# A two-layer decoder trunk in float32: boundaries between sub-layers reordered, matmul operands moved by some bytes, first transfers made smaller

## The chip, the cores and the metric

The kernel runs on one core of one Trainium2 chip. The metric is the device time of one execution in microseconds (us); lower is better.

## The reference

A decoder trunk of two layers over 256 tokens of width 2048, all in float32. Each layer has three sandwich-normalised sub-layers on the residual stream `h`:

```python
for l in range(DEPTH):                                   # DEPTH = 2
    xn = rms_norm(h, mix_pre_g[l])
    proj = jnp.einsum('bsd,dc->bsc', xn, w_in[l])        # 2048 x 4176
    ...                                                  # three groups of heads
    h = h + rms_norm(jnp.einsum('bsc,cd->bsd', mix, w_out[l]), mix_post_g[l])
    xa = memory_attention(rms_norm(h, x_pre_g[l]), rms_norm(mem, mem_g[l]), x_wq[l], x_wkv[l], x_wo[l])
    h = h + rms_norm(xa, x_post_g[l])
    ff = swiglu(rms_norm(h, f_pre_g[l]), f_w_gu[l], f_w_down[l])   # 2048 -> 2 x 5632 -> 2048
    h = h + rms_norm(ff, f_post_g[l])
```

Every weight is used once, so it is read from HBM once (about 445 MB in all).

## The kernel before

**Products.** Each large product is made of three products of float32r operands: an operand is split into `hi` (its rounded copy, ScalarE, L208) and `lo` (the rest, VectorE, L209), and hi*hi, hi*lo and lo*hi are added up in PSUM. There are three forms. `mm_t` (L394) holds 128x128 blocks of weights in TensorE and streams the 256 tokens of the turned activations through them; `mm_w` (L413) does the same for the FFN's hidden layer, with the hi and the lo half of the activations streamed in one instruction of 512 columns for the weights' hi half and 256 columns for their lo half; `mm_n` (L431) holds blocks of activations and streams 256 to 512 columns of weights.

**Weights.** `plan` (L264) lists the weights in the order of use, `loaded` (L320) issues their DMAs on the SP queue into a ring of three raw buffers, `splits` (L337) cuts them into a ring of three hi and three lo tiles, and `prefetch(n)` (L359) issues splits until n of them are ready. `weights` (L372) hands them to the three forms and pumps the side generators after each. With `hold`, in the last block of columns of a closing projection, fewer are issued ahead, so that ScalarE and VectorE come to the closing arithmetic sooner.

**Boundaries.** `project_out` (L653) multiplies into five blocks of output columns (three of 512, two of 256). For each it fetches the gain's slice with a POOL-queue DMA into one of two `gb` buffers; `evac` squares the PSUM tile for the norm's sum and multiplies it by the gain into `og`. The next norm's gain and the turn of the residual stream come in `residual` (L610): `row_rsqrt` (eleven small VectorE instructions), then per pair of 128-column chunks `add` (H += og * r, VectorE), `turn_x` (L587: four TensorE transposes into one PSUM tile `xtp`, and two `split`s with a per-column gain: ScalarE to `xh`, VectorE to `xl`). The next projection starts on the first chunks while the later ones are turned. Three boundaries are *bare*: nothing else is left for TensorE between them (cross-attention to FFN in both layers, FFN to the second layer's mixing). There `warm(n)` (L444) issues n matmuls on constants whose result nobody reads, and `begin` sets a manual schedule (instructions stay in program order on VectorE and ScalarE) until the first block is through.

**Place in memory.** In the built program the turned activations (`x`, `mx`) start at byte 37,248 of each partition, the hi and lo tiles of the weights at 110,976 to 131,456 in steps of 4,096, and the hidden layer `hx` at 153,024. A block of 128 columns is 512 bytes. Below, *distance* means the start of the streamed operand minus the start of the held block that is loaded next, modulo 512 bytes: 0 for `x` and `mx` against weights in either role, and -64 for weights streamed against `hx`.

**Names in the rows.** `raw`, `hi`, `lo`: weights; `acc`: the PSUM tiles of the products; `xtp`: the PSUM tile of a turn; `H`: the residual stream; `og`: the sub-layer's output; `gb`: the slice of gain; `sqj`, `sso`, `ssr`, `rs_r`: squares, their sums and the inverse root; `wz`: constants for `warm`.

Of the kernel before, what the change touches and what calls it, by code (L numbers as in the profile page):

```python
# [58 lines left out]
def trunk(ctx: ExitStack, tc, a, onehot, out):  # L59
# [204 lines left out]
    def plan():  # L264
# [7 lines left out]
        for l in range(L):  # L272
# [8 lines left out]
            yield spec(rows(w_in, C_CU, 512), KD, 512, None if l else [(0, 2), (2, 2), (4, 4), (8, 4), (12, 4)])  # L281
# [305 lines left out]
    def turn_x(src, c, xh, xl, gain):  # L587

        p = ps3.tile([P, 512], F32, tag="tp", name="xtp")
        for j in range(2):  # L590
            for t in range(2):
                nc.tensor.transpose(p[:, j * 256 + t * P:j * 256 + (t + 1) * P],  # L592
                                    src[:, t, (c + j) * P:(c + j + 1) * P], ident)
        for j in range(2):
            split(xh[:, c + j, :], xl[:, c + j, :], p[:, j * 256:(j + 1) * 256], gcol(gain[0], gain[1], c + j, KD))
# [14 lines left out]
    def residual(og, ss, evac, nxt, res, bare):  # L610


        evac()
        r = row_rsqrt(ss)
        if bare:
            warm(24)
        yield
        res["x"] = xh, xl, _ = new_x("x")

        def add(c, n):  # L620
            f = slice(c * P, (c + n) * P)
            for t in range(2):
                nc.vector.scalar_tensor_tensor(H[:, t, f], og[:, t, f], r[:, t:t + 1], H[:, t, f],
                                               op0=ALU.mult, op1=ALU.add)

        add(0, 2)
        turn_x(H, 0, xh, xl, nxt)
        if bare:
            warm(5)
            prefetch(2)  # L630
        yield
        add(2, 2)
# [20 lines left out]
    def project_out(nk, xh, xl, og, gain, add=False, first=None):  # L653


        ss = sm.tile([P, 2, len(TAIL)], F32, tag="sso", name="sso", bufs=2)
        for g, (c0, cols) in enumerate(TAIL):
            last = g == len(TAIL) - 1
            gb = wk.tile([P, 512], F32, tag="gb", name="gb", bufs=2)
            nc.gpsimd.dma_start(gb[:, :cols], gain[c0:c0 + cols].partition_broadcast(P))  # L660
            tiles = mm_n(nk, cols, *(first if first and g == 0 else (xh, xl)), hold=last)

            def evac(tiles=tiles, g=g, c0=c0, cols=cols, gb=gb, last=last):
                for t in range(2):
                    d, p = og[:, t, c0:c0 + cols], tiles[t][:, :cols]
                    if add:
                        nc.vector.tensor_tensor(d, p, d, op=ALU.add)
                        square(d, ss[:, t, g:g + 1])
                        (nc.vector if last else nc.gpsimd).tensor_tensor(d, d, gb[:, :cols], op=ALU.mult)
                    else:  # L670
                        square(p, ss[:, t, g:g + 1])
                        nc.vector.tensor_tensor(d, p, gb[:, :cols], op=ALU.mult)
# [4 lines left out]
    def last_residual(og, ss, evac):  # L677

        evac()
        r = row_rsqrt(ss)  # L680
        for g in range(4):
            for t in range(2):
                f = slice(g * 512, (g + 1) * 512)
                if g == 1:
# [5 lines left out]
                nc.sync.dma_start(out[0, t * P:(t + 1) * P, f], H[:, t, f])  # L690


    def fetch_x(i):
        nc.sync.dma_start(H[:, :, i * 512:(i + 1) * 512],
                          x[0, :, i * 512:(i + 1) * 512].rearrange("(t p) f -> p t f", p=P))

    def initial(res):

        res["x"] = xh, xl, _ = new_x("x")
        for c in range(0, KD, 2):  # L700
            if c % 4 == 0 and 0 < c < 12:
                fetch_x(c // 4 + 1)
# [6 lines left out]
    fetch_x(0)  # L709
    for _ in range(1):  # L710
        in_raw.append(next(loads))
    fetch_x(1)
    for _ in range(2):
        in_raw.append(next(loads))
# [7 lines left out]
    for l in range(L):  # L722
# [352 lines left out]
        mxx = new_x("mx")[2]  # L1075
# [44 lines left out]
        begin(residual(og, oss, evac, ("x_pre_g", l), nx, False), 2, -1)  # L1120
# [37 lines left out]
        def x_turn(s):  # L1158
            t = kp.tile([P, 2, 256], F32, tag="ptX", name="ptX", bufs=4)
# [6 lines left out]
            xt.append(t)  # L1166
# [5 lines left out]
        def x_values(h):  # L1172

            p = ps2.tile([P, 512], F32, tag="lg", name="pvx")
            for j in range(2):
                for k in range(2):
                    mm(p[:, j * 256:(j + 1) * 256], vX[:, k, (h + j) * P:(h + j + 1) * P], xt[h + j][:, k, :],
# [14 lines left out]
        oss, evac = project_out(4, cx[:, 0], cx[:, 1], og, a["x_post_g"][l])  # L1192
        nx = {}
        begin(residual(og, oss, evac, ("f_pre_g", l), nx, True), 3, 0)
# [7 lines left out]
        og = xp.tile([P, 2, D], F32, tag="x", name="og")  # L1202
        nh = FH // P // 2
        for hf in range(2):
# [48 lines left out]
            else:  # L1253
                oss, evac = project_out(nh, hh, hl, og, a["f_post_g"][l], True)
        if l < L - 1:
            cur = {}
            begin(residual(og, oss, evac, ("mix_pre_g", l + 1), cur, True), 3, 0)
# [26 lines left out]
```

## Time and profile before

| | us |
|---|---|
| median of 3 runs | 2496.99 (2495.71 to 2498.8) |
| the profiled execution | 2494.86 |
| its span, first to last instruction | 2493.2 |
| TensorE busy in it | 2435.0 |
| VectorE, ScalarE, POOL busy | 1460.2, 1231.1, 268.8 |
| mean granted TensorE clock | 0.993 |

The profile gives each engine's busy time, its instructions in order of time with the idle time ahead of them and what ended it, and tables of stretches. A matmul's recorded duration runs past the start of the next, since matmuls are pipelined; the pace of a stage is the distance from start to start, which is a stretch divided by the instructions that start in it. A table of stretches also counts the one or two that were begun before the stretch.

### The profile page before, as it was taken

The page shows a single profiled execution, that of the slowest core. Times are in us where ns is not written, and L with a number is a line of the kernel's source. Part 1 is how long each engine was busy: PE and PEld are TensorE (multiplying, and loading weights), DVE is VectorE, ACT ScalarE, POOL GpSimd, SP SyncE. Part 2 cuts the span into 40 slices and gives each one's busy share as a digit, 9 for nine tenths or more (in the row PEclk, how much of TensorE's full clock was granted, in tenths as well). Part 3 has the DMA queues.
Part 4 walks back from the last instruction along what each step waited for, and adds up shares of the span by engine and source line. Part 5 has one row for each costly group of instructions (what it writes and reads, how often), then busy time and mean ns, then how long its engine had stood idle before and what let it go on. Part 6 is the DMA issues. An engine that isn't in the chain of part 4 may idle for free.

```text
span 2493.2 us, 37577 instructions
## 1 busy us (share of the span) xinstructions
PE 2435.0 (98%) x15142; PEld 2170.7 (87%) x15142; DVE 1460.2 (59%) x2272; ACT 1231.1 (49%) x1915; POOL 268.8 (11%) x218
## 2 busy tenths in 40 slices
PE   9999999899999999999989999998999999999997
PEld 8999789888888988888889987998888889888887
DVE  5676767555554455555456767675555544555555
ACT  5655645454444444444355655454544444444443
POOL 0010120001110011111100102200011100111111
PEclk9999999999999999999999999999999999999999
DMA  7654575455555555555644555644555556555564
GB/s 262 216 182 144 188 226 175 132 168 186 186 187 188 189 196 186 186 187 191 206 133 136 183 152 177 217 164 136 169 186 186 187 189 198 187 186 186 186 196 134
DMA packets 362867, 452.95 MB, mean 182 GB/s; under 512 B 8970, under 2 KB 280772, under 8 KB 362692
## 3 DMA queue, kind: packets, MB, share of 16 engines
q1 hardware_dynamic: 360628, 444.23, 54.1%
q0 software_dynamic: 2016, 6.29, 1.3%
q8 instruction: 119, 1.95, 0.3%
q14 instruction: 56, 0.46, 0.1%
q10 hardware_dynamic: 48, 0.02, 0.0%
HBM read 444.72 MB, written 5.79 MB: 181 GB/s over the span
## 4 chain that ended last, share of the span: by engine, by line
PE 79%; issue 11%; DVE 5%; ACT 3%; DMA 1%; POOL 1%; SPq 0%; DVEq 0%; ACTq 0%; POOLq 0%
PE acc L203 75%; DVE lo L209 2%; ACT hi L208 1%; POOL mh L212 1%; DMA gb<-in_x_post_g_dram 1%; ACT sqj L579 1%; PE ixp L203 1%; PE lga L203 0%; ACT x L214 0%; DVE mx L209 0%; PE xtp L592 0%; PE pva L203 0%; DMA H<-in_x_dram 0%; PE pvb L203 0%; DVE x L215 0%
## 5 line engine op out<-in xcount | busy, mean ns | idle before, releaser
L209 DVE TENSOR_TENSOR lo<-raw,hi 128x1024 fp32r<-128x1024 f32 (+2 forms) x838 | 1004.6, 1200 | 808.8 <-ACT hi L208 806.4
L203 PE MATMUL acc<-x,hi 128*128 128x512 f32 (+2 forms) x4800 | 1309.1, 345 | 0.0
L208 ACT ACTIVATE hi<-raw 128x1024 fp32r<-128x1024 f32 (+2 forms) x838 | 858.0, 1026 | 890.2 <-PE acc L203 814.6
L203 PE MATMUL acc<-x,lo 128*128 128x256 f32 x3680 | 995.1, 283 | 21.0 <-DVE lo L209 17.4
L203 PEld LDWEIGHTS acc<-x,hi 128*128 128x128 f32 (+1 forms) x4800 | 828.8, 191 | 109.9 <-issue 2.0
L203 PEld LDWEIGHTS acc<-x,lo 128*128 128x128 f32 x3680 | 699.5, 190 | 38.5 <-DVE lo L209 17.8
L203 PE MATMUL acc<-hi,hx 128*128 128x512 f32 (+1 forms) x1760 | 451.6, 347 | 0.0
L203 PEld LDWEIGHTS acc<-hi,hx 128*128 128x128 f32 x1760 | 304.1, 187 | 49.3
L203 PE MATMUL acc<-lo,hx 128*128 128x512 f32 (+1 forms) x880 | 304.6, 347 | 0.0
L203 PEld LDWEIGHTS acc<-lo,hx 128*128 128x128 f32 x880 | 164.8, 187 | 24.2
L1234 POOL TENSOR_TENSOR u<-u,rbh 128x512 f32<-128x512 f32 x40 | 51.9, 1297 | 1004.3 <-DVE u L429 1004.3
L203 PE MATMUL acc<-hi,mx 128*128 128x512 f32 (+1 forms) x576 | 149.7, 347 | 7.0 <-ACT mx L208 5.2
L203 PEld LDWEIGHTS acc<-hi,mx 128*128 128x128 f32 x576 | 100.4, 191 | 21.0 <-ACT mx L208 6.2
L203 PE MATMUL acc<-hi,x 128*128 128x384 f32 (+1 forms) x384 | 109.0, 359 | 0.0
L1209 POOL TENSOR_TENSOR g<-g,u 128x512 f32<-128x512 f32 x44 | 92.7, 2106 | 135.7 <-ACT g L1219 132.6
L203 PE MATMUL acc<-lo,mx 128*128 128x512 f32 (+1 forms) x288 | 99.1, 344 | 0.0
L214 ACT ACTIVATE x<-xtp,gT 128x256 fp32r<-128x256 f32 x96 | 44.0, 470 | 91.0 <-PE xtp L592 64.0
L203 PEld LDWEIGHTS acc<-hi,x 128*128 128x128 f32 x384 | 70.0, 188 | 6.9 <-issue 2.0
L215 DVE SCALAR_TENSOR_TENSOR x<-xtp,gT,x 128x256 fp32r<-128x256 f32 x96 | 45.1, 481 | 41.4 <-ACT x L214 40.7
L203 PE MATMUL acc<-lo,x 128*128 128x384 f32 (+1 forms) x192 | 68.8, 358 | 0.0
L203 PEld LDWEIGHTS acc<-lo,mx 128*128 128x128 f32 x288 | 54.9, 191 | 6.2
L427 ACT ACTIVATE g<-acc 128x256 f32<-128x256 f32 x80 | 30.4, 380 | 59.4 <-PE acc L203 59.4
(244 smaller groups left out, 2000.2 us busy)
## 6 DMA issues: line engine op xcount, KB each, us to landing
raw<-in_f_w_gu_dram SPq DMA_DIRECT2D x160, 1024.0 KB, 5.0
raw<-in_f_w_down_dram SPq DMA_DIRECT2D x76, 1024.0 KB, 5.0
raw<-in_w_out_dram SPq DMA_DIRECT2D x30, 1024.0 KB, 5.3
raw<-in_w_in_dram SPq DMA_DIRECT2D x50, 512.0 KB, 4.7
raw<-in_w_in_dram SPq DMA_DIRECT2D x23, 1024.0 KB, 5.3
raw<-in_x_wkv_dram SPq DMA_DIRECT2D x16, 1024.0 KB, 4.8
raw<-in_f_w_gu_dram SPq DMA_DIRECT2D x32, 512.0 KB, 4.6
raw<-in_w_in_dram SPq DMA_DIRECT2D x12, 960.0 KB, 5.1
```

Of the source, the lines that this page charges most:

```text
L203: return nc.tensor.matmul(o, lhsT=lhsT, rhs=rhs, start=start, stop=stop, skip_group_check=True)
L208: nc.scalar.activation(hi, src, AF.Copy)
L209: eng.tensor_tensor(lo, src, hi.bitcast(F32), op=ALU.subtract)
L212: nc.gpsimd.tensor_scalar(hi, src, scale, None, op0=ALU.mult)
L214: nc.scalar.activation(hi, src, AF.Copy, scale=scale)
L215: nc.vector.scalar_tensor_tensor(lo, src, scale, hi.bitcast(F32), op0=ALU.mult, op1=ALU.subtract)
L427: nc.scalar.activation(dst[:, b, :], t[:, 256:512], AF.Copy)
L579: nc.scalar.activation(q[:, :src.shape[-1]], src, AF.Square, accum_out=red)
L1209: nc.gpsimd.tensor_tensor(g, g, u, op=ALU.mult)
L1234: nc.gpsimd.tensor_tensor(u, u, two(fnx["rb"]), op=ALU.mult)
```

## The change

1. **Weights ahead.** `hold` leaves two splits ready at the end of a closing projection instead of one; at a bare boundary a third is issued after the adds of chunks 4 to 7.
2. **Closing scales resident.** The gains of the cross-attention's and the FFN's closing norms are fetched whole, into `gX` and `gF`, long ahead. The multiplication of the last block by the gain moves behind the inverse root and the first adds (`rest`); after the FFN it goes to POOL.
3. **A bank per turned chunk.** `turn_x` uses two PSUM tiles of two pools for the two chunks of a pair. The adds of chunks 8 to 15 go to ScalarE (scale) and POOL (add): `add_beside`. The step order changes. `warm(24)` and `warm(5)` become one `warm(38)`.
4. **Operands placed.** `new_x` takes an offset; `x` then starts that many bytes below the distance 0 to the weights: 32 for the mixing and cross-attention inputs, 0 for `mx`, 256 (first layer) and 128 (second layer) for the FFN input. A gap of 448 bytes and `gF` put `hx` at distance 0.
5. **First transfers.** The first fetch of x is 256 columns instead of 512, the first weights one block of rows instead of two (then three).
6. `ptX` tiles share the `mp` buffers; the last residual adds run by token half, and one output DMA is issued from ScalarE.

```diff
-            yield spec(rows(w_in, C_CU, 512), KD, 512, None if l else [(0, 2), (2, 2), (4, 4), (8, 4), (12, 4)])
+            yield spec(rows(w_in, C_CU, 512), KD, 512, None if l else [(0, 1), (1, 3), (4, 4), (8, 4), (12, 4)])
...
-                prefetch(3 if not hold else 1 if n == nk else 2 if n + len(subs) >= nk else 3)
+                prefetch(3 if not hold or n < nk else 2)
...
-    def new_x(nm):
-        x = xp.tile([P, 2, KD, S], F32R, tag="xx", name=nm)
+    def new_x(nm, off):
+        f = 2 * KD * S
+        x = xp.tile([P, f + 72], F32R, tag="xx", name=nm)[:, 72 - off // 4:72 - off // 4 + f]
+        x = x.rearrange("p (a k t) -> p a k t", a=2, k=KD)
...
-        p = ps3.tile([P, 512], F32, tag="tp", name="xtp")
-        for j in range(2):
+        for j, (pool, tag) in enumerate(((ps3, "tp"), (ps2, "lg"))):
+            p = pool.tile([P, 512], F32, tag=tag, name="xtp")
...
     residual:
-        evac()
+        rest = evac()
         r = row_rsqrt(ss)
         if bare:
-            warm(24)
+            warm(38)
...
+        def add_beside(c, n):
+            f = slice(c * P, (c + n) * P)
+            for t in range(2):
+                nc.scalar.activation(og[:, t, f], og[:, t, f], AF.Copy, scale=r[:, t:t + 1])
+                nc.gpsimd.tensor_tensor(H[:, t, f], H[:, t, f], og[:, t, f], op=ALU.add)
         add(0, 2)
         turn_x(H, 0, xh, xl, nxt)
         if bare:
-            warm(5)
             prefetch(2)
-        yield
         add(2, 2)
+        rest()
+        yield
         turn_x(H, 2, xh, xl, nxt)
-        yield
-        for c in range(4, KD, 4):
-            add(c, 4)
+        add(4, 4)
+        if bare:
+            prefetch(3)
+        yield
+        turn_x(H, 4, xh, xl, nxt)
+        add_beside(8, 4)
+        yield
+        turn_x(H, 6, xh, xl, nxt)
+        yield
+        turn_x(H, 8, xh, xl, nxt)
+        add_beside(12, 4)
+        yield
+        for c in range(10, KD, 2):
             turn_x(H, c, xh, xl, nxt)
-            yield
-            turn_x(H, c + 2, xh, xl, nxt)
             yield
...
     project_out, the last block:
-                        (nc.vector if last else nc.gpsimd).tensor_tensor(d, d, gb[:, :cols], op=ALU.mult)
+                        if not last:
+                            nc.gpsimd.tensor_tensor(d, d, gb, op=ALU.mult)
...
-        res["x"] = xh, xl, _ = new_x("x")
+        res["x"] = xh, xl, _ = new_x("x", 32)
...
+        gX = kp.tile([P, D], F32, name="gX")
+        nc.gpsimd.dma_start(gX, a["x_post_g"][l].partition_broadcast(P))
...
-        begin(residual(og, oss, evac, ("f_pre_g", l), nx, True), 3, 0)
+        begin(residual(og, oss, evac, ("f_pre_g", l), nx, True, (256, 128)[l]), 3, 0)
...
+        nc.gpsimd.memset(fp.tile([P, 112], F32, name="gap"), 0.0)
+        gF = fp.tile([P, D], F32, name="gF")
+        nc.gpsimd.dma_start(gF, a["f_post_g"][l].partition_broadcast(P))
```

**Where instructions move.** On VectorE, at the first layer's boundary from cross-attention to FFN (`gb` and `gX`: the gain; `sso`: sums of squares; `lo`: a split of the FFN's weights), before:

```order
L672 TENSOR_TENSOR og<-acc,gb 128x256
L209 TENSOR_TENSOR lo<-raw,hi 128x1024
L672 TENSOR_TENSOR og<-acc,gb 128x256 x3
L584 TENSOR_REDUCE ssr<-sso 128x2
L499 TENSOR_SCALAR rs_v<-ssr 128x2
```

and with the change:

```order
L693 TENSOR_TENSOR og<-acc,gX 128x256
L209 TENSOR_TENSOR lo<-raw,hi 128x1024
L693 TENSOR_TENSOR og<-acc,gX 128x256
L209 TENSOR_TENSOR lo<-raw,hi 128x1024
L587 TENSOR_REDUCE ssr<-sso 128x2
L499 TENSOR_SCALAR rs_v<-ssr 128x2
```

The last block's two multiplications have left the place ahead of the reduction, and a second split of the next weights stands there.

On the same engine behind the inverse root, where the residual stream is added up (`H`) and turned (`x`), before:

```order
L623 SCALAR_TENSOR_TENSOR H<-og,rs_r,H 128x256 x2
L215 SCALAR_TENSOR_TENSOR x<-xtp,gT,x 128x256 x2
L209 TENSOR_TENSOR lo<-raw,hi 128x1024
L623 SCALAR_TENSOR_TENSOR H<-og,rs_r,H 128x256 x2
L215 SCALAR_TENSOR_TENSOR x<-xtp,gT,x 128x256 x2
L623 SCALAR_TENSOR_TENSOR H<-og,rs_r,H 128x512 x2
L215 SCALAR_TENSOR_TENSOR x<-xtp,gT,x 128x256 x2
L209 TENSOR_TENSOR lo<-raw,hi 128x1024 x2
```

and with the change:

```order
L624 SCALAR_TENSOR_TENSOR H<-og,rs_r,H 128x256 x2
L215 SCALAR_TENSOR_TENSOR x<-xtp,gT,x 128x256 x2
L624 SCALAR_TENSOR_TENSOR H<-og,rs_r,H 128x256 x2
L703 TENSOR_TENSOR og<-acc,gX 128x256 x2
L215 SCALAR_TENSOR_TENSOR x<-xtp,gT,x 128x256 x2
L624 SCALAR_TENSOR_TENSOR H<-og,rs_r,H 128x512 x2
L209 TENSOR_TENSOR lo<-raw,hi 128x1024
L215 SCALAR_TENSOR_TENSOR x<-xtp,gT,x 128x256 x2
```

The split between the first two turns is gone (it was made earlier), the two multiplications by the gain come here, and of the two splits in a row ahead of the fourth turn one comes ahead of the third.

On TensorE at the same boundary, before:

```order
L203 MATMUL acc<-hi,cx 128x256
L448 MATMUL warm<-wz 128x256 x24
L592 MATMUL xtp<-ident,H 128x128 x4
L448 MATMUL warm<-wz 128x256 x5
L203 MATMUL acc<-x,lo 128x256
```

and with the change:

```order
L203 MATMUL acc<-hi,cx 128x256
L448 MATMUL warm<-wz 128x256 x38
L595 MATMUL xtp<-ident,H 128x128 x4
L203 MATMUL acc<-x,lo 128x256
```

The constants' matmuls stand in one group ahead of the first turn, and nothing stands between that turn and the first product.

## Rows read from the trace of the kernel before

**Rows 1.** The page's part 1: busy time, share, instructions of each engine.

```profile
PE 2435.0 (98%) x15142; PEld 2170.7 (87%) x15142; DVE 1460.2 (59%) x2272; ACT 1231.1 (49%) x1915; POOL 268.8 (11%) x218
```

**Rows 2.** Timeline, first boundary to the FFN: start, duration, engine, operation [idle <-releaser].

```profile
474.75 3.04 PE L448 MATMUL warm<-wz 128*128 128x256 f32 x24
...
477.91 0.75 DVE L672 TENSOR_TENSOR og<-acc,gb 128x256 f32<-128x256 f32 x2 [2.67 <-DMA gb<-in_x_post_g_dram]
...
480.69 0.88 DVE L623 SCALAR_TENSOR_TENSOR H<-og,rs_r,H 128x256 f32<-128x256 f32 x2
481.32 0.85 PE L592 MATMUL xtp<-ident,H 128*128 128x128 f32 x4 [3.53 <-DVE H L623]
...
482.73 0.47 PE L203 MATMUL acc<-x,lo 128*128 128x256 f32 x1
```

**Rows 3.** Timelines of PE, ACT and DVE further on at that boundary.

```profile
491.33 1.04 PE L592 MATMUL xtp<-ident,H 128*128 128x128 f32 x8
495.83 0.39 PE L203 MATMUL acc<-x,lo 128*128 128x256 f32 x1 [3.46 <-DVE lo L209]
...
519.56 0.39 PE L203 MATMUL acc<-x,lo 128*128 128x256 f32 x1
519.78 0.28 PE L203 MATMUL acc<-x,hi 128*128 128x256 f32 x1
...
520.50 0.28 PE L203 MATMUL acc<-x,hi 128*128 128x256 f32 x1
...
493.10 0.47 ACT L214 ACTIVATE x<-xtp,gT 128x256 fp32r<-128x256 f32 x1 [0.55 <-DVE x L215]
493.47 1.99 ACT L208 ACTIVATE hi<-raw 128x1024 fp32r<-128x1024 f32 x2
...
494.55 2.36 DVE L209 TENSOR_TENSOR lo<-raw,hi 128x1024 fp32r<-128x1024 f32 x2 [0.46 <-ACT hi L208]
```

**Rows 4.** Table of stretches: from:to, us, PE busy (instructions), granted clock, DMA share, GB/s.

```profile
482.90:486.20 3.30, 3.30 (x16) 0.50 0.00 0
```

**Rows 5.** PE's timeline at the other two bare boundaries: `warm`, and the second block's start.

```profile
1237.51 3.04 PE L448 MATMUL warm<-wz 128*128 128x256 f32 x24
...
1281.07 0.39 PE L203 MATMUL acc<-x,lo 128*128 128x256 f32 x1
...
1715.51 1.72 PE L448 MATMUL warm<-wz 128*128 128x256 f32 x13
...
1760.61 0.38 PE L203 MATMUL acc<-x,lo 128*128 128x256 f32 x1
```

**Rows 6.** Table of stretches: five stages at a steady pace.

```profile
1575.10:1589.30 14.20, 14.20 (x64) 1.00 0.76 232
842.00:867.00 25.00, 25.00 (x223) 1.00 0.65 206
350.00:370.00 20.00, 20.00 (x169) 1.00 0.72 225
760.00:830.00 70.00, 70.00 (x302) 1.00 0.53 182
550.00:700.00 150.00, 150.00 (x860) 1.00 0.57 189
```

**Rows 7.** PE's groups by line and form: count, busy us, mean ns.

```profile
L203 PE MATMUL acc<-x,hi 128*128 128x512 f32 x2560 | 889.9, 396 | 0.0
L203 PE MATMUL acc<-x,hi 128*128 128x256 f32 x2176 | 414.6, 288 | 0.0
L203 PE MATMUL acc<-hi,hx 128*128 128x512 f32 x1056 | 331.8, 394 | 0.0
```

**Rows 8.** Timelines of the first product and of the end, by engine.

```profile
9.51 0.35 PE L203 MATMUL acc<-x,lo 128*128 128x256 f32 x1 [1.30 <-DVE lo L209]
...
2479.48 0.97 DVE L669 TENSOR_TENSOR og<-og,gb 128x256 f32<-128x256 f32 x2 [0.29 <-ACT sqj L579]
...
2483.33 3.42 POOL L686 TENSOR_TENSOR H<-H,og 128x512 f32<-128x512 f32 x2 [15.55 <-ACT og L685]
```

More of the change, by code (lines that the diff above doesn't have):

```diff
@@ L587, in turn_x @@
     def turn_x(src, c, xh, xl, gain):
-        p = ps3.tile([P, 512], F32, tag="tp", name="xtp")
-        for j in range(2):
+        for j, (pool, tag) in enumerate(((ps3, "tp"), (ps2, "lg"))):
+            p = pool.tile([P, 512], F32, tag=tag, name="xtp")
             for t in range(2):
[L592 to L595, printed above, removed]
+                nc.tensor.transpose(p[:, t * P:(t + 1) * P], src[:, t, (c + j) * P:(c + j + 1) * P], ident)
+            split(xh[:, c + j, :], xl[:, c + j, :], p[:, 0:256], gcol(gain[0], gain[1], c + j, KD))
     def pre_norm(res):
@@ L658, in project_out @@
             last = g == len(TAIL) - 1
-            gb = wk.tile([P, 512], F32, tag="gb", name="gb", bufs=2)
-            nc.gpsimd.dma_start(gb[:, :cols], gain[c0:c0 + cols].partition_broadcast(P))
+            if gain.shape[0] == P:
+                gb = gain[:, c0:c0 + cols]
+            else:
+                gb = wk.tile([P, 512], F32, tag="gb", name="gb", bufs=2)[:, :cols]
+                nc.gpsimd.dma_start(gb, gain[c0:c0 + cols].partition_broadcast(P))
             tiles = mm_n(nk, cols, *(first if first and g == 0 else (xh, xl)), hold=last)
@@ L668, in evac, with rest @@
                         square(d, ss[:, t, g:g + 1])
-                        (nc.vector if last else nc.gpsimd).tensor_tensor(d, d, gb[:, :cols], op=ALU.mult)
+                        if not last:
+                            nc.gpsimd.tensor_tensor(d, d, gb, op=ALU.mult)
                     else:
                         square(p, ss[:, t, g:g + 1])
-                        nc.vector.tensor_tensor(d, p, gb[:, :cols], op=ALU.mult)
+                        if not last:
+                            nc.vector.tensor_tensor(d, p, gb, op=ALU.mult)
+                if not last:
+                    return
+                def rest():
+                    for t in range(2):
+                        d, p = og[:, t, c0:c0 + cols], tiles[t][:, :cols]
+                        if add:
+                            nc.gpsimd.tensor_tensor(d, d, gb, op=ALU.mult)
+                        else:
+                            nc.vector.tensor_tensor(d, p, gb, op=ALU.mult)
+                return rest
             if last:
@@ L677, in last_residual @@
     def last_residual(og, ss, evac):
-        evac()
+        rest = evac()
         r = row_rsqrt(ss)
[L681 to L684, printed above, removed]
+        rest()
+        for t in range(2):
+            for c0, n, beside in ((512, 512, True), (0, 512, False), (1024, 512, False), (1536, 512, False)):
+                f = slice(c0, c0 + n)
+                if beside:
                     nc.scalar.activation(og[:, t, f], og[:, t, f], AF.Copy, scale=r[:, t:t + 1])
@@ L689, in last_residual, with fetch_x @@
                                                    op0=ALU.mult, op1=ALU.add)
[L690 to L695, printed above, removed]
+                (nc.scalar if t and beside else nc.sync).dma_start(out[0, t * P:(t + 1) * P, f], H[:, t, f])
+    def fetch_x(c0, n):
+        nc.sync.dma_start(H[:, :, c0:c0 + n], x[0, :, c0:c0 + n].rearrange("(t p) f -> p t f", p=P))
     def initial(res):
-        res["x"] = xh, xl, _ = new_x("x")
+        res["x"] = xh, xl, _ = new_x("x", 32)
         for c in range(0, KD, 2):
             if c % 4 == 0 and 0 < c < 12:
-                fetch_x(c // 4 + 1)
+                fetch_x((c // 4 + 1) * 512, 512)
             turn_x(H, c, xh, xl, ("mix_pre_g", 0))
@@ L708, in trunk @@
     next(g0)
[L709 to L714, printed above, removed]
+    fetch_x(0, 256)
+    in_raw.append(next(loads))
+    fetch_x(256, 256)
+    in_raw.append(next(loads))
+    fetch_x(512, 512)
+    in_raw.append(next(loads))
     warm(12)
```

22 lines of the change are left out of this document (12 added, 10 removed).

## The prediction

> **What bounds the kernel now.** The page's part 1 comes first: TensorE is busy for 2435.0 of 2493.2 us [rows 1], and no other engine for 60% of the span. So time can come from two places only: the stretches in which TensorE stands still or runs at half clock, and the pace of its matmuls where it runs without a gap.
>
> The standing time is found in the timeline of a bare boundary [rows 2]. At the first one, real work ends at 474.75, where the 24 warm matmuls begin. VectorE then waits 2.67 us for the gain's slice, still on its way by DMA, multiplies for 0.75, and the eleven small instructions of the inverse root and the first adds follow. TensorE waits 3.53 us for H, turns, runs five more warm matmuls, and the first product starts at 482.73: 7.98 us after the warm start. Further on it waits again, 3.46 us from the second pair of turns to 495.83, for a `lo` that is split only then [rows 3]: ScalarE and VectorE had the turned chunks first, and there each copy of a second chunk waits for VectorE on the first (0.55 us), because both lie in one PSUM tile. The table of stretches shows the clock at 0.50, the 1.2 of the two levels 1.2 and 2.4 GHz, right behind the idle time [rows 4]. From the warm start to the second block's first product, 519.56, 44.8 us pass for 192 matmuls [rows 2, 3]. These run at 0.12 us each, six starts from 519.78 to 520.50 [rows 3], so they need 23.0 us. The other two boundaries take 43.6 and 45.1 us [rows 5].
>
> The pace is read from stretches without idle time, less the two instructions begun before each [rows 6]. Hidden layer by down weights, 512 columns (distance -64): 70 us by 300, 233 ns. The same with 256 columns: 25 us by 221, 113 ns. Output projection, distance 0: 512 columns 14.2 us by 62 or 63, about 227 ns; 256 columns 20 us by 167, 120 ns. The FFN's pair of 512 and 256 columns, distance 0: 150 us by 429 pairs, 350 ns. The same instruction differs by up to 7 ns from place to place at full clock, and in opposite senses for 512 and 256 columns.
>
> **The change part by part.**
>
> *Start of a bare boundary (parts 1 to 3).* With the gain resident the wait of 2.67 us goes, and with the multiplications moved 0.75 us more. What is late next: a second split, 1.2 us of VectorE (half of the 2.36 of two [rows 3]), now stands ahead of the reduction, and the squares must be done. I let the reduction start at 476.5, two microseconds earlier than now (477.91 + 0.75 = 478.66). The inverse root takes 2.1 us (478.6 to 480.69 [rows 2]) and the way from there to the first turn 0.63, so H is ready for it at 479.2. The 38 warm matmuls take 38 by 0.12 = 4.6 us and end at 479.4, which is level with it. From the turn's start to the first product it is now 1.41 us with five warm matmuls between [rows 2]; without them and with a copy that starts after two transposes, 1.0. First product: 480.4 instead of 482.73.
>
> *The rest of the first block.* Two splits are ready and the third is issued before it is needed, so the wait of 3.46 us goes, and with both waits the half clock behind them: two such stretches at this boundary, each worth half its 3.4 us. What is left is 23.0 us of products, seven more turns of four transposes at 0.5 (eight in 1.04 [rows 3]), 3.5, and some 0.7 us for each of the first two turns, whose chunks are still being added up: 27.9 us, so 508.3 against 519.56, a gain of 11.2. By the same steps the second boundary, which waits for no DMA and gains only 0.9 at its start, ends 9.7 earlier, and the third 11.5 [rows 5]. The sum is 32.4; I take off 0.1 us for each of the 24 handovers: **-30**. Ends: half of it, -15, if the split's turn on ScalarE and VectorE stays what products wait for, and -36 with no wait left at the early turns.
>
> *POOL's adds.* Four adds of 512 columns at each boundary at 1.71 us [rows 8] are 6.8 us on POOL, wanted some 10 us after their inputs are there: nothing. If they slow VectorE beside them, 2 us at each of three boundaries: ends 0 and +6. The fetches of gX and gF stand ahead of them on POOL's queue, but in memory that is long free.
>
> *First transfers (part 5).* The first product waits for `lo`, at 9.51 [rows 8]. Half the bytes come first and the split is half as wide: about 0.6 us each on ScalarE and VectorE for 1.1 to 1.2. The following blocks come no sooner. **-1.5**, ends -2.5 and +0.5. *End (part 6).* The inverse root need not wait for two multiplications (from 2479.48, 0.97 us [rows 8]); the squares end about 0.4 before them: **-0.4**, ends -1 and +1, since POOL takes their place.
>
> *hx at distance 0 (part 4).* 1056 hi and half as many lo products of 512 columns [rows 7], 1584 by (227 - 233) ns, are -9.5 us. The tail's two blocks of 256 against three of 512 make 1056 of those, by (120 - 113), +7.4. **-2**, ends 0 and -9.5.
>
> *x off distance 0 (part 4).* The trace has no row of -32, 128 or 256. `mm_t`: 2176 hi products and half as many lo, 3264 of 256 columns [rows 7], of which about 3000 leave distance 0. Nearest rows: 120 ns at 0, 113 at -64 (with the roles exchanged); I take the middle, -3.5 ns: **-10**, ends 0 and -21. `mm_w`: 2560 pairs [rows 7]. At best 227 + 113 = 340 ns, at worst 233 + 120 = 353, now 350. I take 347, a little over the middle: **-7**, ends -25 and +8. `mm_n` on x (some 550 instructions of 384 and 512 columns): nothing, ends -4 and +4.
>
> Here a rule speaks against the change. The rows say that the same streamed block takes 113 or 120 ns by where it lies [rows 6]. The Trainium skill, "TensorE: Matmul & The Clock Gate", section "Step-by-step: what each phase is for", gives TensorE two independent SBUF read ports and says that loading the next tile's weights "doesn't steal SBUF read bandwidth from the running matmul". By that rule the place of an operand is worth nothing and the sum lacks the last three terms; the rows disagree with it, unless the difference comes from something else in those stages, and that is the first rival.
>
> The sum: -30 - 1.5 - 0.4 - 2 - 10 - 7 = -50.9 from the profiled execution's 2494.86, which is 2.1 under the median shown: **2444 us**.
>
> **The rivals.** *Placement does nothing.* The 7 ns between stages would come from what else runs there, not from the distance. For: stages also differ in DMA load, 0.53 to 0.76 [rows 6], and in which operand is held. Against: 512 columns go the other way than 256 within the same stages. Only the boundaries, the start and the end remain, -31.9: 2463.
>
> *The boundaries give half.* The third split needs a buffer of the ring of three, which is free only when the first split's products are through; the wait for `lo` comes back, shorter, at the next pair. For: ScalarE and VectorE each work 2.3 to 2.4 us for two chunks (a split, two copies), near TensorE's 3.4. Against: that is still less. -15 - 1.9 - 19 = -35.9: 2459.
>
> *Slower: the FFN's pair loses.* The hidden layer streams two runs of 256 columns, 16 KB apart, and the offsets 256 and 128 were tried in no row. Each ns on the pair costs 2.56 us. With -44 from the rest the pair must rise by 17 ns, to 367, for no change; at 372 (every matmul of it as much above the slowest rows as those are above the fastest) it is 2494.9 - 44 + 56 = 2507. For: the two lengths go in opposite senses. Against: no row is that slow.
>
> *Placement does more.* Both forms go to their best rows, 113 ns and 340: 2494.9 - 33.9 - 21 - 25 = 2415.
>
> That the change does not do what it says is excluded by the order of its instructions.
>
> **How the numbers follow.** Forecast 0.48, placement nothing 0.22, half the boundaries 0.13, more 0.11, the FFN's pair loses 0.06. A measurement of this kernel tells 0.2%, 5 us, from no change. All but the last lie clearly below; of the mixed ends (half the boundaries and a small loss of pace) I put 0.03 within 5 us. Faster 0.92, same 0.03, slower 0.05. The range reaches from the best case, 2414, past "placement nothing" and some loss of pace with it, 2475: what lies outside is the last rival, half the boundaries without any gain of pace, and both placements at their best with a boundary better than I have it.
>
> **What would show it.** Right: some 5.7 us from a bare boundary's warm start to its first product and 33 to 34 to the second block's first; no wait for `lo` of 3 us; no or little half clock there. 227 and 120 ns in the hx products; less than 120 in `mm_t`, less than 350 in the FFN's pair. Wrong: if the hx products stay at 233 and 113, distance is not the cause; if the first block still takes 40 us, the weights are not ahead; if the pair is over 353, the offsets are badly put.

## Result and the profile after the change

| | before | after |
|---|---|---|
| median, us | 2497.26 (2495.71 to 2498.8, 4 runs) | 2463.19 (2460.3 to 2463.72, 4 runs) |
| profiled execution, us | 2494.86 | 2460.3 |
| its span, us | 2493.2 | 2458.6 |

The ratio is 0.9861, 95% interval 0.9844 to 0.9878: 34 us faster. The forecast said 2444 with a range of 2414 to 2475; the time lies in the range, 19 us above the forecast, and within 1 us of the first rival, "placement does nothing". One execution of a kernel below (*Weights not ahead*) had a mean granted clock of 0.555 and took 4006.84 us; that kernel's times are given without it.

Part 1 of the page after, to be held against [rows 1]:

```profile
PE 2419.2 (98%) x15169; PEld 2170.7 (88%) x15169; DVE 1456.6 (59%) x2249; ACT 1240.9 (50%) x1936; POOL 296.8 (12%) x228
```

TensorE lost 15.8 us of busy time. POOL gained 28.0: the adds of chunks 8 to 15 take 34.6, and it fetches fewer slices of gains. ScalarE gained 9.8, VectorE lost 3.6. The rest of the 34.6 us by which the span is shorter, 18.8, is idle time of TensorE that is gone.

**The first boundary.** Timelines of the changed kernel by engine (start, duration, engine, operation, [idle before <-releaser]), against [rows 2, 3]:

```profile
477.71 4.72 PE L448 MATMUL warm<-wz 128*128 128x256 f32 x38
482.27 0.60 PE L595 MATMUL xtp<-ident,H 128*128 128x128 f32 x4
...
483.33 0.39 PE L203 MATMUL acc<-x,lo 128*128 128x256 f32 x1 [0.46 <-ACT x L214]
...
495.25 0.44 PE L595 MATMUL xtp<-ident,H 128*128 128x128 f32 x2 [0.30 <-POOL H L631]
...
512.16 0.28 PE L203 MATMUL acc<-x,lo 128*128 128x256 f32 x1
...
478.97 0.16 DVE L587 TENSOR_REDUCE ssr<-sso 128x2 f32<-128x10 f32 x1
...
484.89 0.75 DVE L703 TENSOR_TENSOR og<-acc,gX 128x256 f32<-128x256 f32 x2
```

The squares' sum (L587) no longer waits for the gain: the multiplication (L703) comes six microseconds behind it. The first product starts 5.62 us after the warm start (7.98 before), the second block 34.45 (44.8 before). No wait of 3.46 us for `lo` is left; the longest is 0.74, at 496.43. The half clock of [rows 4] is gone with the idle time, as the first row of the second table below shows.

**Stretches.** A table of stretches gives for TensorE: from:to, us, busy (instructions), granted clock, DMA share, GB/s. First the kernel before (cross-attention from its first memory product to the warm start; then the three bare boundaries, each from the warm start to the first product of the next kind, with FFN, mixing and FFN behind it; the second half of the FFN's hidden layer, second layer; 480 `mm_t` products of the mixing, with 101 smaller instructions between them that are the same in every kernel):

```profile
371.87:474.75 102.88, 102.88 (x782) 1.00 0.48 161
474.75:746.58 271.83, 261.17 (x1603) 0.99 0.54 177
1237.51:1324.90 87.39, 77.94 (x607) 0.96 0.49 153
1715.51:1987.63 272.12, 261.80 (x1603) 0.98 0.54 176
2109.96:2356.23 246.27, 246.27 (x1410) 1.00 0.57 188
158.92:232.03 73.11, 73.11 (x582) 1.00 0.53 161
```

Then the same places after, with the stretch behind the first product ahead of them and the two kinds of `hx` products behind:

```profile
483.30:486.20 2.90, 2.87 (x24) 1.00 0.04 13
374.02:477.71 103.69, 102.48 (x782) 1.00 0.46 159
477.71:737.16 259.45, 257.27 (x1613) 1.00 0.56 186
1226.31:1303.46 77.15, 73.87 (x616) 1.00 0.53 169
1694.84:1954.56 259.72, 257.51 (x1612) 1.00 0.56 185
2076.00:2323.04 247.04, 247.04 (x1411) 1.00 0.57 188
161.10:233.57 72.47, 72.47 (x582) 1.00 0.53 163
737.16:826.92 89.76, 89.76 (x398) 1.00 0.56 191
826.92:858.60 31.68, 31.68 (x266) 1.00 0.60 192
```

The ledger, after minus before: the three boundaries -12.4, -10.2 and -12.4, so -35.0. Cross-attention +0.8 in each layer (the second layer's stretch is 102.88 and 103.69 too). The `hx` products of a half take 89.8 + 31.7 = 121.4 us instead of 92.4 + 29.9 = 122.3 (396 and 264 at the paces of [rows 6]): -3.6 over four halves. The hidden layer's second half 0.0 and +0.8. All up to the first memory product +2.15 (its starts are 371.87 and 374.02 in the second rows). These make -34.0; the rest, to -34.6, is nearly all the end.

**Two places that got worse.** In the cross-attention, the changed kernel's timelines of PE, DVE and POOL at 382 to 388 us:

```profile
381.63 6.96 POOL L631 TENSOR_TENSOR H<-H,og 128x512 f32<-128x512 f32 x4 [3.80 <-ACT og L630]
...
383.44 1.77 DVE L624 SCALAR_TENSOR_TENSOR H<-og,rs_r,H 128x512 f32<-128x512 f32 x1
385.13 2.31 DVE L209 TENSOR_TENSOR lo<-raw,hi 128x1024 fp32r<-128x1024 f32 x1
...
387.59 0.36 PE L203 MATMUL acc<-mh,lo 128*128 128x256 f32 x1 [1.21 <-DVE lo L209]
```

An add of VectorE and a split take 1.77 and 2.31 us while POOL adds, and TensorE waits for the `lo` tile behind them. And at the start, TensorE's waits in the changed kernel:

```profile
9.10 0.39 PE L203 MATMUL acc<-x,lo 128*128 128x256 f32 x1 [1.05 <-ACT x L214]
...
12.27 0.96 PE L595 MATMUL xtp<-ident,H 128*128 128x128 f32 x7 [1.50 <-DMA H<-in_x_dram]
...
69.45 0.39 PE L203 MATMUL acc<-x,lo 128*128 128x256 f32 x1 [0.70 <-DVE lo L209]
...
106.84 0.39 PE L203 MATMUL acc<-kvn,lo 128*128 128x256 f32 x1
```

The first product comes 0.41 us earlier than [rows 8] have it. The second fetch of x is then waited for, and at 69 us a split stands behind VectorE's work on the lambda constants (small products of the input `a_lambda`). TensorE's waits before 107 us add up to 7.3 us, where they were 5.3, and the first `kvn` product starts 2.2 us later than in the kernel before (104.63).

### The profile page after: what moved, and what is told of

It is laid out like the page before. It is cut to its first block, busy times and chain, and to the rows that moved or that the text cites. A ratio compares the mean times of both kernels' runs of the same rounds, so it can differ in the third digit from the quotient of the medians.

```text
span 2458.6 us, 37634 instructions
## 1 busy us (share of the span) xinstructions
PE 2419.2 (98%) x15169; PEld 2170.7 (88%) x15169; DVE 1456.6 (59%) x2249; ACT 1240.9 (50%) x1936; POOL 296.8 (12%) x228
## 4 chain that ended last, share of the span: by engine, by line
PE 93%; DVE 3%; DMA 1%; ACT 1%; issue 0%; SPq 0%; DVEq 0%; ACTq 0%
PE acc L203 89%; DVE lo L209 1%; PE ixp L203 1%; PE xtp L595 1%; PE lga L203 0%; DVE mx L209 0%; ACT hi L208 0%; DVE H L624 0%; DMA H<-in_x_dram 0%; PE warm L448 0%; PE pva L203 0%; DMA m<-in_mem_dram 0%; PE pvb L203 0%; PE lgx L203 0%; PE pvx L203 0%
## 5 line engine op out<-in xcount | busy, mean ns | idle before, releaser
L203 PEld LDWEIGHTS acc<-x,hi 128*128 128x128 f32 (+1 forms) x4800 | 818.6, 188 | 107.7 <-issue 2.0
L203 PEld LDWEIGHTS acc<-x,lo 128*128 128x128 f32 x3680 | 691.6, 188 | 23.0 <-ACT x L214 9.7
L427 ACT ACTIVATE u<-acc 128x256 f32<-128x256 f32 x80 | 30.4, 379 | 58.5 <-PE acc L203 58.5
```

The source lines that it names most:

```text
L203: return nc.tensor.matmul(o, lhsT=lhsT, rhs=rhs, start=start, stop=stop, skip_group_check=True)
L427: nc.scalar.activation(dst[:, b, :], t[:, 256:512], AF.Copy)
```

## Experiments

The theory after the result: the boundaries brought all of the gain, placement nothing but the `hx` products, and POOL's adds took something back. The rival: placement brings what the forecast gave it, and the boundaries brought half. Times below are medians with the kernel before beside them (2496.8 to 2497.5), and stretches as above. The profiled execution was the fastest of its runs for the changed kernel and three of the variants, and the slowest for two, so stretches are compared with stretches and medians with medians.

### Placement undone

```diff
-begin(residual(og, oss, evac, ("f_pre_g", l), nx, True, (256, 128)[l]), 3, 0)
+begin(residual(og, oss, evac, ("f_pre_g", l), nx, True, 0), 3, 0)
...
-nc.gpsimd.memset(fp.tile([P, 112], F32, name="gap"), 0.0)
+nc.gpsimd.memset(fp.tile([P, 96], F32, name="gap"), 0.0)
```

The three offsets of 32 become 0 likewise.

> Only the placement is undone: x, mx and the FFN input at distance 0, hx at -64 again; boundaries, start and end as changed. Theory 1, the gain is that of the boundaries and the placement is worth the 3.6 us of the hx products alone: 2463 + 3 = about 2466 us, hx at 233 and 113 ns, second half of the FFN's mm_w products 246.3 us in both layers as in both kernels. Theory 2, placement gives the 10 to 19 us of the forecast and the boundaries only some 18: 2473 to 2482 us.

2457.92 us (2457.54 to 2459.52), ratio 0.9843 (0.9828 to 0.9858): no slower without the placement. Its interval overlaps that of the changed kernel, so the 5 us between the medians don't show it to be faster. One thing in the expectation is wrong: the shorter gap does not put `hx` back to -64 but on the other side, to +64. There its products ran as at no place before (512 columns, then 256):

```profile
739.47:830.12 90.65, 90.65 (x398) 1.00 0.55 189
830.12:860.04 29.92, 29.92 (x265) 1.00 0.64 203
```

That is 120.6 us in a half, where distance 0 gave 121.4 and -64 122.3. The second layer's hidden half went back from 247.04 to 246.27. With `hx` at -64 the four halves would take 7 us more, by an estimate from these stretches (122.3 - 120.6 each), which makes some 2465 us, where theory 1 has 2466. Theory 2 falls: 10 to 19 us of placement are not there.

### The adds of chunks 8 to 15 back on VectorE

```diff
 def add_beside(c, n):
-    for t in range(2):
-        nc.scalar.activation(og[:, t, f], og[:, t, f], AF.Copy, scale=r[:, t:t + 1])
-        nc.gpsimd.tensor_tensor(H[:, t, f], H[:, t, f], og[:, t, f], op=ALU.add)
+    add(c, n)
```

> The residual adds of chunks 8 to 15 go back to VectorE everywhere (no ScalarE scale, no POOL add). Theory 1, POOL's adds slow VectorE beside them, and that is what the cross-attention lost: from the last mx product to the first warm matmul 102.9 us as before the change, not 103.7, in both layers, and the lo splits beside the boundary at 1.2 us where one took 2.2; the bare boundaries then either gain the 1.5 us waited at chunks 8 and 9 or lose up to 3 us each for VectorE's four extra adds of 0.74 us. In all 2459 to 2470 us. Theory 2, the cross-attention's loss has another cause (the gain's fetch, another order): it stays at 103.7 us.

2456.55 us (2453.9 to 2458.39), ratio 0.9835 (0.9821 to 0.985). Cross-attention and first boundary, in the table of stretches:

```profile
375.16:477.40 102.24, 102.24 (x782) 1.00 0.49 161
477.40:735.49 258.09, 256.94 (x1613) 1.00 0.57 187
```

VectorE's timeline at that boundary, then POOL's and VectorE's of the changed kernel at the same place:

```profile
492.06 1.40 DVE L624 SCALAR_TENSOR_TENSOR H<-og,rs_r,H 128x512 f32<-128x512 f32 x2
493.38 1.22 DVE L209 TENSOR_TENSOR lo<-raw,hi 128x1024 fp32r<-128x1024 f32 x1
```

```profile
492.67 2.52 POOL L631 TENSOR_TENSOR H<-H,og 128x512 f32<-128x512 f32 x2 [5.74 <-ACT og L630]
497.24 2.12 POOL L631 TENSOR_TENSOR H<-H,og 128x512 f32<-128x512 f32 x1 [2.04 <-ACT og L630]
...
494.11 2.17 DVE L209 TENSOR_TENSOR lo<-raw,hi 128x1024 fp32r<-128x1024 f32 x1 [1.65 <-ACT hi L208]
...
496.99 1.21 DVE L209 TENSOR_TENSOR lo<-raw,hi 128x1024 fp32r<-128x1024 f32 x1
498.12 0.86 DVE L215 SCALAR_TENSOR_TENSOR x<-xtp,gT,x 128x256 fp32r<-128x256 f32 x2
```

With four more adds of its own at each boundary VectorE is through sooner: its last `xl` split ends 28.7 us after the warm start at the first boundary, 30.1 in the changed kernel. The gain is 1.45 us in each cross-attention and 1.3 to 1.4 at each of the three boundaries, 6.9 in all: that is what POOL's help cost. The run takes out ScalarE's scaling together with POOL's adds, and at the bare boundaries the two are not told apart; in the cross-attention TensorE's wait of 1.21 us stands behind the slowed rows of VectorE and is gone here. Instructions whose two tensor inputs both lie in SBUF slow down beside POOL: an add of 128x512 takes 0.70 us here and took 1.77 in the cross-attention above, a split of weights 1.22 here and 2.17 and 2.31 there. The two `xl` splits at 498.12, with one input in PSUM, took 0.86 for both in the middle of POOL's work, no more than the 0.88 they take elsewhere. Which of the two began first decides who is slowed. Of the sixteen splits of weights that ran beside these adds, the three begun ahead of the add kept 1.21 us, as at 496.99, and there the add took 2.12, where those that meet no split take 1.3; the thirteen begun behind it took 1.23 to 2.31. The Trainium skill, "SBUF — State Buffer", section "Who interferes with whom", says so: a VectorE instruction with two SBUF inputs contends with a GpSimd instruction that reads SBUF, and the second one waits. By that rule the adds were not free, and the trace agrees.

### Weights not ahead

```diff
-prefetch(3 if not hold or n < nk else 2)
+prefetch(3 if not hold else 1 if n == nk else 2 if n + len(subs) >= nk else 3)
...
 add(4, 4)
-if bare:
-    prefetch(3)
```

> Splits ahead undone: one split ready at the end of the closing projection and no third split after the adds of chunks 4 to 7; all else as changed. Theory 1, the wait for lo at the second pair of turns is what the first block lost: each bare boundary is longer by 5 to 9 us, with a wait for lo of 2 to 3.5 us at the second pair, 2478 to 2490 us. Theory 2, the separate banks and the moved multiplications carry the gain: 0 to 3 us a boundary, below 2472 us.

2473.69, 2474.79 and 2478.14 us, ratio 0.9916 (0.9896 to 0.9936). The first boundary's stretch:

```profile
478.31:742.28 263.97, 259.00 (x1612) 0.99 0.56 182
```

TensorE's longest wait in it, from its timeline, with the row ahead of it:

```profile
491.17 1.03 PE L595 MATMUL xtp<-ident,H 128*128 128x128 f32 x8
494.83 0.44 PE L595 MATMUL xtp<-ident,H 128*128 128x128 f32 x2 [2.63 <-POOL H L631]
```

4.5, 4.0 and 4.5 us are lost (81.19 and 264.18 at the others), 13.0 in all: below theory 1 and above theory 2. The wait does not come back at `lo`, either. POOL's adds of chunks 8 and on begin 15.2 us after the warm start, 15.0 in the changed kernel, so they are hardly late. But the third split comes at 494.94 (489.45 in the changed kernel), and until then TensorE has no products to run between the turns of chunks 4 to 7 and that of chunk 8 (the changed kernel runs 24 there, from 491.60 to 494.57): it comes to the turn at once and stands there for H. The products behind the waits then run at a granted clock of 0.50, the 1.2 GHz level, 0.21 us from start to start where 0.12 is usual.

### One bank for a pair

```diff
-for j, (pool, tag) in enumerate(((ps3, "tp"), (ps2, "lg"))):
-    p = pool.tile([P, 512], F32, tag=tag, name="xtp")
+p = ps3.tile([P, 512], F32, tag="tp", name="xtp")
...
```

> turn_x puts both chunks of a pair into one PSUM tile again; all else as changed. Theory 1, the copy of a second chunk that waits 0.5 us for VectorE lies on TensorE's path at each of the eight pairs: 3 to 4 us more at each bare boundary (warm start to the first hx product 262 to 263 us where the changed kernel has 259.5), some 2474 us in all. Theory 2, VectorE's own load sets the pace of a boundary and a ScalarE wait costs nothing: under 1 us each, 2463 to 2466 us.

2479.98 us, ratio 0.9931 (0.9917 to 0.9944). The first boundary's stretch:

```profile
479.82:744.18 264.36, 258.61 (x1612) 1.00 0.56 182
```

ScalarE's timeline in it:

```profile
499.69 0.47 ACT L214 ACTIVATE x<-xtp,gT 128x256 fp32r<-128x256 f32 x1 [2.26 <-DVE x L215]
```

4.9, 5.2 (82.37) and 5.0 us (264.71), more than theory 1 had it. The copy of a second chunk waits for VectorE not only 0.55 us as in [rows 3] but up to 2.26, because VectorE may have a split of weights ahead of the first chunk's `lo`; ScalarE's own splits queue behind that copy. The split in question (497.11) took 2.16 us beside POOL's adds; behind one that took 1.23 (501.14) the wait is 1.32. So a part of this price is POOL's.

### Gains fetched late

```diff
-oss, evac = project_out(4, cx[:, 0], cx[:, 1], og, gX)
+oss, evac = project_out(4, cx[:, 0], cx[:, 1], og, a["x_post_g"][l])
...
-rest = evac()
+evac()
 r = row_rsqrt(ss)
```

> Closing gains fetched slice by slice again, and the last block multiplied by the gain ahead of the inverse root, as in the kernel before (after the FFN on POOL, where that kernel used VectorE); all else as changed. Theory 1, the forecast's: the wait of 2.67 us for the slice and 0.75 us of multiplications come back ahead of the first turn at both cross-attention boundaries and 0.9 at the other: 3.4 + 3.4 + 0.9 = some 8 us, 2471 us. Theory 2, a part of it is covered, since the splits issued ahead now stand before the reduction: 3 to 5 us in all, 2466 to 2468 us.

2470.06 us, ratio 0.9894 (0.988 to 0.9907). Stretches of the first and third boundary:

```profile
480.35:743.78 263.43, 259.07 (x1612) 0.99 0.56 182
1700.34:1966.10 265.76, 260.36 (x1612) 0.99 0.56 181
```

The third's waits, from the timelines of VectorE and TensorE:

```profile
1704.96 0.76 DVE L699 TENSOR_TENSOR og<-acc,gb 128x256 f32<-128x256 f32 x2 [3.28 <-DMA gb<-in_x_post_g_dram]
...
1708.37 1.09 PE L595 MATMUL xtp<-ident,H 128*128 128x128 f32 x4 [3.31 <-DVE H L624]
```

4.0 and 6.0 us at the boundaries behind the cross-attention, -0.3 at the other (76.88), which never waited for a slice: 9.8, at two of the three places that theory 1 named and a little above its 8. The profiled execution was the slowest of four; the medians lie 6.9 us apart. At the third boundary the first products behind the wait run at a granted clock of 0.50, which is a part of its 6.0.

### First transfers wide again

```diff
-[(0, 1), (1, 3), (4, 4), (8, 4), (12, 4)]
+[(0, 2), (2, 2), (4, 4), (8, 4), (12, 4)]
...
-fetch_x(0, 256)
+fetch_x(0, 512)
...
```

> The first transfers as in the kernel before: 512 columns of x and two blocks of rows of weights. Theory 1, the narrow ones bring the first product 0.4 us forward and pay for it with a wait of 1.8 us behind the first block; the start of the mixing's mm_n products (118.8 us in the changed kernel, 116.6 before) comes 0 to 1.5 us earlier with the wide ones, and the rest of the 2.2 us is the lambda constants' work, which the new order of instructions puts between two splits. Theory 2, the narrow transfers gain the 1.5 us of the forecast and other things lose 3.7: then the wide ones bring it to 120 us.

2462.59 us (2462.1 to 2462.96). TensorE's first product and first `kvn` product:

```profile
9.52 0.55 PE L203 MATMUL acc<-x,lo 128*128 128x256 f32 x1 [1.30 <-DVE lo L209]
...
106.61 0.39 PE L203 MATMUL acc<-kvn,lo 128*128 128x256 f32 x1
```

Between these two executions the narrow transfers bring 0.42 us at the first product and nothing by 106 us (106.84 with them). Neither is shown to be theirs: in the other kernels with narrow transfers the first product starts anywhere from 8.76 to 10.38, and the `kvn` product from 106.95 to 108.98. The 2 us behind the kernel before (104.63) are there in both, so the transfers alone don't cause them. Waits at the lambda work are a part of them; what moved that work was not tried.

### Other places

```diff
-begin(residual(og, oss, evac, ("f_pre_g", l), nx, True, (256, 128)[l]), 3, 0)
+begin(residual(og, oss, evac, ("f_pre_g", l), nx, True, (64, 32)[l]), 3, 0)
...
-hx = fp.tile([P, 2, nh, S], F32R, tag="hx", name="hx")
+ho = ((416, 320), (192, 0))[l][hf] // 4
+hx = fp.tile([P, 2 * nh * S + 128], F32R, tag="hx", name="hx")[:, ho:ho + 2 * nh * S]
```

The other inputs' offsets change in the same way, and the gap goes. In the first expectation the sign of the places of `hx` and `mx` is again the opposite of what was run: weights minus `hx` was 32, 128, 256 and -64, weights minus `mx` 64 and 32.

> Other places in memory only. hx at distance -32 and -128 (first layer, first and second half) and 256 and 64 (second layer); x at -64 and -48 (mixing, first and second layer), -16 and -96 (cross-attention), -64 and -32 (FFN); mx at -64 and -32. Theory 1, the pace follows the distance whichever operand is held: mx at -64 like hx was, 233 and 113 ns; mm_t at -64 at 113 ns, some 3 us less in 480 products; -32 between the two at 230 and 117; FFN pair at -64 113 + 233 = 346 ns or less, 6 us less over a half. Theory 2, only held activations follow it: mx at -64 at 233 and 113, but mm_t stays at 117 to 120 ns and the FFN's pair at 350 to 352 ns wherever x lies.

> Other places only. Weights minus hx 48 and 80 (first layer), 96 and -192 (second); mx 48 and 96; mixing input -80 and -96, cross-attention -64 and -80, FFN -192 and -16. If only multiples of 64 give full steps, hx at 48, 80 and 96 lies between the values at 32, 64 and 128 (512 columns 229 to 233 ns, 256 columns 113 to 119), -192 reads like 64 and not like 256; mm_t at -80 and -96 is slower than at -64 (over 71.3 us for 480 products); the FFN's pair at -192 and -16 is 350 ns or more, since no place tried so far beat 350.

2469.35 and 2466.6 us, one run each. Two stretches of the first (480 `mm_t` products at -64; the first layer's hidden half with x at -64), and the first of these at -80 in the second:

```profile
161.78:233.06 71.28, 71.28 (x581) 1.00 0.54 166
858.87:1107.30 248.43, 248.43 (x1411) 1.00 0.57 187
```

```profile
161.12:234.03 72.91, 72.91 (x582) 1.00 0.54 163
```

`hx` products, ns each (a stretch divided by its 396 or 264 products):

| weights minus `hx` | -64 | 0 | 32 | 48 | 64 | 80 | 96 | 128 | 256 | -192 |
|---|---|---|---|---|---|---|---|---|---|---|
| 512 columns | 233.3 | 226.7 | 233.3 | 231.8 | 228.9 | 230.0 | 233.3 | 232.4 | 226.8 | 228.9 |
| 256 columns | 113.4 | 120.0 | 116.7 | 116.7 | 113.3 | 118.1 | 120.0 | 118.6 | 120.0 | 117.8 |

Stretches with x streamed, us (the first has 101 other instructions in it):

| x minus weights | 0 | -16 | -32 | -48 | -64 | -80 | -96 | -128 | -192 | -256 |
|---|---|---|---|---|---|---|---|---|---|---|
| 480 `mm_t` | 73.11 | | 72.47 | 72.82 | 71.28 | 72.91 | 72.26 | | | |
| hidden half (704 pairs) | 246.27 | 248.26 | 248.43 | | 248.43 | | | 247.04 | 246.91 | 246.27 |

The held `mx` follows the table at 32 (22.40 us for 192 products of 256 columns, 116.7 ns) but not at 64 (22.62 us, 117.8 ns, where `hx` has 113.3). The place counts for streamed x too, against theory 2 of the first sweep: `mm_t` is best at -64, 1.8 us for 480 products. But the pair is best at 0 and at -256, and theory 1's gain of 6 us at -64 is a loss of 2.2.

### Two versions that put this together

`best1` has VectorE's adds, x at -64 (mixing, cross-attention) and 0 (FFN), `mx` at 32 and `hx` at 64. `best2` has `hx` at 0 again and the narrow blocks' own place. The diffs to the changed kernel, of `best1` and then of what `best2` has besides:

```diff
-begin(residual(og, oss, evac, ("x_pre_g", l), nx, False, 32), 2, -1)
+begin(residual(og, oss, evac, ("x_pre_g", l), nx, False, 64), 2, -1)
...
-nc.gpsimd.memset(fp.tile([P, 112], F32, name="gap"), 0.0)
+nc.gpsimd.memset(fp.tile([P, 96], F32, name="gap"), 0.0)
```

```diff
-hi = ws.tile([P, 1024], F32R, tag="hi", name="hi")
+hi = ws.tile([P, 1024], F32R, tag="hi", name="hi")[:, place:]
...
-yield spec(rows(wd, c0, n), nh, n)
+yield spec(rows(wd, c0, n), nh, n, None, 3 if n == 256 else None, 16 if n == 256 else 0)
```

> The changed kernel with the adds of chunks 8 to 15 on VectorE, the FFN input at distance 0, the mixing and cross-attention inputs at -64, mx at 32 and hx at 64 (weights minus hx). By the stretches measured so far: 6.9 us from the adds, 3.5 from hx, 0.8 from the second layer's FFN, 1.2 us for 480 mm_t products at -64 instead of -32 in each layer, 0.6 for mx in each: 2463 - 15 = about 2448 us. If the parts overlap or the total follows the order of instructions instead, 2453 to 2458 us.

> As the version before (best1), but hx at distance 0, where its 512-column products took 226.7 ns, and the weights of the down projection's two narrow blocks 64 bytes further in their tiles, so that those 256-column products see 64 (113.3 ns). To make room they are split three blocks of rows at a time instead of four. If the pace follows the distance of the very instruction: 89.8 and 29.9 us in each half instead of 90.7 and 29.9, 3.5 us less in all, 2444 us. If the smaller splits (a fourth of the products per handover less) become the wait, or the narrow products follow something else than this distance: 31.7 us or more, 2448 to 2452 us.

`best1`: 2447.54 us (2446.35 to 2447.95), ratio 0.9801 (0.9788 to 0.9815), 15.6 us under the changed kernel, and within 1 us of the 2448 that the stretches of the runs above add up to. The stretch of its first boundary (the one with 480 `mm_t` products took 71.28 us):

```profile
477.98:736.08 258.10, 256.96 (x1613) 1.00 0.57 187
```

`best2`: 2446.95 us (2445.53 to 2447.34), the same. Its two kinds of `hx` products:

```profile
734.78:824.54 89.76, 89.76 (x398) 1.00 0.57 191
824.54:855.64 31.10, 31.10 (x265) 1.00 0.59 186
```

The wide blocks have their 226.7 ns; the narrow ones take 117.8 at the same 64 bytes at which they took 113.3 when `hx` had been moved instead of the weights. It is not a wait where one split hands over to the next: 252 of the 263 steps from start to start are 117 to 119 ns. `mx` at 64 had 117.8 as well, and there nothing was split smaller. The distance modulo 512 bytes is therefore not all that counts; what else does was not found.

## Why the prediction came out as it did

- **Start of a bare boundary and its first block (-30): right.** First product 5.62 us after the warm start at the first and third (5.7 forecast), second block after 34.3 to 35.7 (33 to 34). At the middle one the start brought nothing: 7.11 where 6.84 had been, since TensorE waits 1.12 us for H behind the warm matmuls. To the second block the three gain 10.4, 7.9 and 10.8 us, 29.0. Behind it they gain 1.6 to 2.4 us more, which the forecast left out: at the first boundary 1.4 of it are two waits of 0.7 us for `lo` (at 523.40 and 527.22 in the kernel before). Taken away alone, weights ahead cost 13.0, a bank per chunk 15.1 and resident gains 9.8 us. That is 37.9, more than the 35.0 of all together, so the parts overlap. What the longer `warm(38)` does by itself was not tried.
- **POOL's adds (0, ends 0 and +6): wrong, they cost 6.9.** Two mistakes. The step priced them only at the bare boundaries, though the mixing's `residual` runs them too (2.9 of the 6.9); and it took the lower end. The trace before had a row against it, in the view of the tile `H` (least, median and longest ns), for the six adds of VectorE at the kernel's end, where POOL adds beside them:

```profile
L688 DVE SCALAR_TENSOR_TENSOR H<-og,rs_r,H x6: 739/747/1748, 2482.6 to 2487.9; 128x512 f32<-128x512 f32 x6
```

- **`hx` at distance 0 (-2): right, -3.6.** 226.7 and 120.0 ns, where the forecast had 227 and 120; with the unrounded 6.6 ns both ways, 1584 products gain 10.5 and 1056 lose 7.0.
- **`mm_t` off distance 0 (-10): mis-sized.** The middle between two rows was taken for a place that neither of them showed. At -32 480 products gain 0.64 us, 1.3 ns each, where 3.5 were taken. At -64 the same products gain 1.83, 3.8 ns each: the nearest row's place would have brought the term, the place chosen did not. In the totals even the 0.64 us is lost among waits: the second layer's mixing, from its first `cqh` product (1303.46) to the first memory product (1591.15), took 287.69 us, and 287.73 in the kernel before (1324.90 to 1612.63).
- **The pair (-7): wrong, 0 and +0.8.** At -256 nothing changes, at -128 it is 1 ns slower; none of the six places tried beat 0.
- **First transfers (-1.5): wrong, nothing.** The step priced the wait for `lo` alone. With `lo` early the first product waits for ScalarE's copy of the turned chunk instead (9.10, `ACT x`) and comes only 0.41 us sooner (in the other kernels with narrow transfers between 0.75 sooner and 0.87 later), and then TensorE waits 1.50 for the second fetch of x.
- **End (-0.4): right**, some 0.5 by the ledger. What no step had: the 2 us of new waits before 107 us.

Against the profiled execution, 2460.3, the sum was 16 us too low. That is the two placement terms; the other errors (boundaries -5, `hx` -1.6, start +3.7, cross-attention +1.6) nearly cancel, which is luck. So the part of the forecast that was read from the boundaries' waits held, the part that carried a pace over to places not yet measured did not, and the time lies in the range because the range was made to hold "placement does nothing". The median lies 3 us above that execution. "Placement does nothing" has the right total, with another cause: the place does matter, by up to 7 ns an instruction, but the places chosen bring little. The products of `hx` take 113 to 120 and 227 to 233 ns by nothing but an offset. The Trainium skill, "TensorE: Matmul & The Clock Gate", section "Step-by-step: what each phase is for", has the load of the next weights take no read bandwidth from the running matmul; taken to mean that the offset is worth nothing, as the forecast took it, the trace disagrees. Whether loads and streams get in each other's way, or something else makes the difference, no run here shows. The slower rival is out, since the pair stayed at 350 to 351 ns (246.27 and 247.04 us by 704). Its price was also summed wrongly: the slowest rows, raised by what they stand above the fastest, make 239 + 127 = 366 ns and not 372. By the same sum that is 2492 us and not 2507, no slower than the kernel before.

## What to carry to other kernels

Before an add is moved from VectorE to POOL, look at the VectorE instructions that will run beside it: those with two SBUF inputs take up to 2.4 times their time here when they begin behind the add, and the one TensorE waits for may be among them. Give each chunk that two engines read in turn a PSUM tile of its own, and price a bank by the longest queue of the engine that is waited for, not by one copy. A pace read at one place in memory says nothing of a place between: measure the place itself, several in one run.

## Unexpected of the hardware

- TensorE's pace by the place of its operands is neither smooth nor of one sign: 512 columns run at 226.7 ns at 0 and 256 bytes and at 233.3 at 32, 96 and -64; 256 columns at 113.3 at 64, 120.0 at 0, 96 and 256.
- VectorE beside POOL's adds: 128x512 from 0.74 to 1.77 us, 128x1024 splits from 1.22 to 2.31. A split begun ahead of the add keeps 1.21, and the add takes 2.12 instead of 1.3.
